# The head of a hybrid decoder step: rows of x scaled in place and turned by plain transposes, with another order of loads and of work

## The chip, the cores and the metric

The kernel runs on one core of a Trainium2 chip. Its engines run side by side, each through its own list in order: TensorE (PE, matrix products; PEld is its loading of stationary operands), VectorE (DVE), ScalarE (ACT), GpSimd (POOL) and SyncE (SP, which here only issues DMA transfers). The metric is the device time of one execution in microseconds (us). A profile shows one execution, with times counted from its span's start.

## The reference

One layer of a decoder on 1024 prompt rows and 8 x 8 sample rows, 1088 rows (T) of 1024 features in all. What matters here is its first part:

```python
mod = silu(c) @ w_ada + b_ada
shift, scale, gate = split(mod, 3)
h = rmsnorm(x, norm_g) * (1 + scale) + shift
proj = h @ w_in          # [u_pool | z_pool | z_ssm | xBC | dt | g]
...
x = x + gate * ((sigmoid(g_pool) * P + sigmoid(g_ssm) * S) @ w_o)
```

`c` has nine rows: one for the prompt and one for each of eight samples. P and S are the results of a pooling branch and a state-space branch, which take nearly all of the time and which the change leaves as they are.

## The kernel before

**Layout.** The work runs with features on partitions: h is held as eight tiles of 128 features by 1088 rows. The rows of x arrive as nine blocks (eight of 128 rows, and one of the 64 sample rows), so they are turned on the way. The blocks form three groups (XG), {0, 1}, {2, 3, 4} and {5 to 8}, with 256, 384 and 448 columns (BLK). "Feature k" below is a tile of 128 features, "group" one of these three sets of columns.

**The head**, `first()`, L838, does the following, and `in_line` (L340) pins the instructions of all five engines to the order in which the code writes them.
- x_load (L194) loads a block. x_square (L200) sums its squares, on DVE (L204) or ACT (L206). x_root (L208) takes the root of a group's mean squares on ACT, and x_unit (L212) the reciprocal rs on DVE; it then makes a diagonal matrix of each block's rs (L219, 128x128, DVE).
- x_turn (L223) multiplies a block of x, the stationary operand, by that diagonal, which scales and turns it in one fp32 product (L231), once per block and feature: 72 products. x_copy (L235) takes the result from PSUM to the tile `tf`, DVE for even features (L239) and ACT for odd ones (L241).
- ada_load, ada_mm, ada_out and ada_end (L252 to L300) make shift and scale, `md`, from w_ada in three parts: part 0 is for features 0 and 1, part 1 for 2 and 3, part 2 for 4 to 7. Each part is 64 products (L277), a copy on ACT (L284), transposes (L292) and sums on DVE (L296, L299).
- h_make (L309) forms h in a rounded high and a low half: hi on ACT (L323, for the sample columns L332), the scaled copy on DVE or ACT (L327, L325), low on DVE (L315).
- w_split (L850) splits a first weight tile into a high half (ACT, L163) and a low half (L166: on POOL, or on DVE where `V` is given). products (L856) multiplies it with h, three products per feature and tile (L866 to L868), into banks for the gates of columns t = 0 and 1.
- gate_bias and gate_load issue the loads for the last gate: a memset of bg on POOL (L827), four loads behind it on SP (L829), then weights (L817). gate_mm (L823) uses them.

**Behind the head.** `combine` (L466) makes the sums of h's quarters that the next products, a Strassen-like scheme (L595 to L597), use: three sums on DVE (L497 to L499), a rounding on ACT (L500), a low half on DVE (L493), for four features. `pair_w` (L527) does the like for weights: two loads (L529), differences on DVE (L540), splits on ACT and on DVE or POOL (L163, L166). `next(wst)` runs it one step on; its first step in the head holds two L540. `done` (L872) takes sigmoids of the gate columns on ACT (L875) and stores them, dt_block (L727, L730) the dt columns.

**What sets the order.** The written order within `first`; behind it a scheduler with priorities. SP issues loads in order as well, and a transfer waits for the one eight before it. PSUM tiles of kind "ps" come from five banks, those of kind "mm" from three.

Of the kernel before, what the change touches and what calls it, by code (L numbers as in the profile page):

```python
# [10 lines left out]
AF = mybir.ActivationFunctionType  # L11
ALU = mybir.AluOpType
# [8 lines left out]
P = 128  # L21
D = 1024
KT = D // P
# [30 lines left out]
def tile_pool_ssd_step(  # L54
# [6 lines left out]
    nc = tc.nc  # L61
# [37 lines left out]
    def R(shape=(P, T), dt=F32):  # L99
        return hs.tile(list(shape), dt, tag="R", name=nm("R"), bufs=3)  # L100
# [4 lines left out]
    def PB():  # L105
        return psB.tile([P, 512], F32, tag="ps", name=nm("ps"))
# [4 lines left out]
    def const(shape, name, dt=F32):  # L111
        return cp.tile(shape, dt, tag=name, name=name)
# [26 lines left out]
        nc.gpsimd.memset(rc[:, t:t + 1], 1.0 / (t + 1))  # L139


    c9 = const([P, KT, NB + 1], "c9")
    store_(c9, c_all)

# [8 lines left out]
    def c_turn():  # L153
        act(scT[:, :, 0:9], c9, AF.Silu)

    def v_turn():
        V.tensor_scalar(vT[:, 8:16], vT[:, 8:16], 1.0, None, ALU.add)
# [27 lines left out]
    xr = []  # L185
# [1 line left out]
    ss = const([P, 9], "ss")  # L187
    nc.gpsimd.memset(ss, 1.0)
    rs = const([P, 9], "rs")
    dg = []  # L190
    hh_ = [None] * KT
    hl_ = [None] * KT

# [6 lines left out]
    def x_square(i, eng):  # L200
        xt, n = xr[i]
        sqj = pa.tile([P, D], F32, tag="rawA", name=nm("sqj"), bufs=5)
        if eng is V:
            V.scalar_tensor_tensor(sqj[:n], xt[:n], 1.0, xt[:n], ALU.mult, ALU.mult, accum_out=ss[:n, i:i + 1])  # L204
        else:
            act(sqj[:n], xt[:n], AF.Square, accum_out=ss[:n, i:i + 1])  # L206

    def x_root(a, b):  # L208
        n = xr[a][1]
        act(rs[:n, a:b], ss[:n, a:b], AF.Sqrt, bias=eps[:n], scale=1.0 / D)  # L210

    def x_unit(a, b):  # L212
        n = xr[a][1]
        V.reciprocal(rs[:n, a:b], rs[:n, a:b])
        if not dg:
            dg.append(R())
        for i in range(a, b):
            n = xr[i][1]
            V.tensor_scalar(dg[0][:n, i * P:i * P + n], ident[:n, :n], rs[:n, i:i + 1], None, ALU.mult)  # L219

    tf = [None] * KT

    def x_turn(g3, k):  # L223

        if g3 == 0:
            tf[k] = tfp.tile([P, T], F32, tag="tf", name=nm("tf"), bufs=8)
        px = PB()
        c = 0
        for i in range((0, *XG)[g3], XG[g3]):
            xt, n = xr[i]  # L230
            mm(px[:, c:c + n], xt[:n, k * P:(k + 1) * P], dg[0][:n, i * P:i * P + n], start=True, stop=True)  # L231
            c += n
        return g3, k, px, c

# [8 lines left out]
    def x_turns(g3, ks):  # L243
        for k in ks:
            x_copy(x_turn(g3, k), nc.scalar if k % 2 else V)
# [6 lines left out]
    def ada_load(part, k):  # L252
        a, b = PARTS[part]
        w = (b - a) * P
        if part == 0:
            if k == 0:
                wtile[0] = Y4(hp, F32)
            t = wtile[0][:, k // 2, :D]
        else:
            if part == 2 or k % 2 == 0:  # L260
                wtile[part, k] = G((P, D))
            t = wtile[part, k if part == 2 else k - k % 2]
        if part == 2:
            load(t, w_ada[8 + k])
        else:
            if k % 2 == 0:
                load(t, w_ada[4 * part + k // 2])
            t = t[:, k % 2 * 512:k % 2 * 512 + 512]
        wraw[part, k] = t.rearrange("p (s c) -> p s c", s=2)
# [568 lines left out]
    def first():  # L838
        ET = mybir.EngineType
        every = (ET.PE, ET.Activation, ET.DVE, ET.Pool, ET.SP)  # L840
        in_line(every, True)
        raws = {}

        def w_load(t, j):
            raws[t, j] = raw_()
            load(raws[t, j], w_first[t, j].rearrange("p (k c) -> p k c", c=P))

        w = {}

        def w_split(t, j, eng=None):  # L850
            w[t, j] = split(raws[t, j], eng=eng)

        banks = {}

        def products(bi, ks):
            o, n = BLK[bi]  # L856
            for t in range(2):
                if (bi, t) not in banks:
                    banks[bi, t] = (PB if (bi, t) in ((1, 1), (2, 0), (2, 1)) else PA)()[:, :n]
            for k in ks:  # L860
                for t in range(2):
                    ps = banks[bi, t]
                    hi, lo = w[t, k // 4]
                    a, b = hi[:, k % 4, :], lo[:, k % 4, :]
                    rh, rl = hh_[k][:, o:o + n], hl_[k][:, o:o + n]
                    mm(ps, a, rh, start=(k == 0), stop=False)  # L866
                    mm(ps, b, rh, start=False, stop=False)
                    mm(ps, a, rl, start=False, stop=(k == KT - 1))  # L868

        tags = iter(("s1", "u2", "u3", "c2", "s1", "u2"))  # L870

        def done(bi, t):  # L872
            o, n = BLK[bi]
            buf = pa.tile([P, HF], F32, tag=next(tags), name=nm("g0"))
            act(buf[:, :n], banks[bi, t], AF.Sigmoid)  # L875
            store_(gs_d[t][:, o:o + n], buf[:, :n])

        for i in range(9):
            x_load(i)
        for k in range(KT):  # L880
            if k == KT - 2:
                w_load(0, 0)
                w_load(1, 0)
            ada_load(0, k)
        for k in range(KT):
            ada_load(1, k)
        for k in range(4):
            ada_load(2, k)
        late = late_loads()

        x_square(0, V)
        x_square(1, V)
        c_turn()
        x_root(0, 2)
        x_unit(0, 2)
        x_square(2, None)
        x_square(3, V)
        x_turns(0, range(2))
        x_square(4, None)
        x_turns(0, range(2, 4))  # L900
        x_root(2, 5)
        x_unit(2, 5)
        x_turns(0, range(4, 8))
        x_square(5, V)
        x_square(6, None)
        x_turns(1, range(4))
        x_square(7, V)
        x_square(8, None)
        x_turns(1, range(4, 6))
        x_root(5, 9)  # L910
        x_unit(5, 9)
        x_turns(1, range(6, 8))
        v_turn()
        x_turns(2, range(4))
        for k in range(6):
            ada_mm(0, k)
        x_turns(2, range(4, 5))
        w_split(0, 0)
        w_split(1, 0)
        ada_mm(0, 6)  # L920
        ada_mm(0, 7)
        mr = ada_out(0)
        x_turns(2, range(5, 6))
        ada_end(0, mr)
        turned = [x_turn(2, k) for k in (6, 7)]

        h_make(0, range(2))
        products(0, range(2))
        x_copy(turned[0], V)
        x_copy(turned[1], nc.scalar)  # L930
        h_make(1, range(2))
        for k in range(KT):
            ada_mm(1, k)
        products(1, range(2))
        h_make(2, range(2))
        w_load(0, 1)
        w_load(1, 1)
        for k in range(4, 8):
            ada_load(2, k)
        next(late)  # L940
        mr = ada_out(1)
        products(2, range(1))
        ada_end(1, mr)
        products(2, range(1, 2))

        for bi in range(2):
            h_make(bi, range(2, 4))
            products(bi, range(2, 4))
        h_make(2, range(2, 4))
        w_split(0, 1, V)  # L950
        w_split(1, 1, V)
        for k in range(KT):
            ada_mm(2, k)
        mr = ada_out(2)
        products(2, range(2, 3))
        ada_end(2, mr)
        products(2, range(3, 4))
        dtw = dt_w()
        run, (wz, wst) = light[0][1], light[0][0]()
        bg = gate_bias()  # L960
        for k in range(4):
            gate_load(k)
        next(wst)

        for bi in range(3):
            h_make(bi, range(4, 8))
        for bi in range(3):
            products(bi, range(4, 8))
            for k in range(2 * bi, min(2 * bi + 2, 4)):
                gate_mm(k)  # L970
                gate_load(k + 4)

        sums = combine()
        next(late)
        for bi in range(3):
            done(bi, 0)
            done(bi, 1)
            next(sums)
        dt_block(dtw, 0)
        dt_block(dtw, 1)  # L980
        next(sums)
        next(wst)
        dt_block(dtw, 2)
        next(sums)
        for k in range(4, 8):
            gate_mm(k)
        gate_end(bg)
        next(late, None)

        def hook(n):  # L990
            if n in (0, 2):
                next(wst)
            if n < 2:
                next(sums)
            if n in (3, 4):
                next(wst)
                next(sums)
        run(wz, hook)
        in_line(every)
# [1082 lines left out]
```

## Time and profile before

| | before |
|---|---|
| median of 3 runs | 1242.26 us (1239.66 to 1242.32) |
| span of the profiled execution | 1238.8 us |
| PE busy in 0 to 9 us | 0.00 us |
| PE busy in 20 to 40 us | 19.92 us |
| PE busy in 40 to 60 us | 18.44 us |
| PE busy in 77 to 100 us | 21.36 us |
| first turned block on PE (L231) | 9.29 us |
| shift and scale of part 0 on DVE (L296) | 30.37 us |
| first products of features 2 and 3 (L866) | 40.85 us |
| first large product (L595) | 77.73 us |

The profile gives the span of the one profiled execution; the time of a run lies some us above it. In a row of the timeline stand the start, the duration, the engine, the line, the operation and its tiles; a number x6 behind it says that several like instructions are joined, and the bracket gives the idle time of the engine ahead of the row and what ended it. A matmul's duration includes its way through the array, so that two in a row overlap; their pace is read from the starts. Rows of stretches give busy time and count, the granted clock of PE, the DMA share and GB/s. An fp32 product makes two records.

### The profile page before, as it was taken

Reading aid. Unit: us, or ns where it says so; the run is one execution under the profiler, and the core shown is the slowest. Engines: PE = TensorE matmul, PEld = TensorE weight load, DVE = VectorE, ACT = ScalarE, POOL = GpSimd, SP = SyncE. Lnnn points to the kernel's source line nnn. Section 1 sums busy time; section 2 is a strip of 40 time slices with the busy share of each in tenths; the row PEclk is TensorE's granted clock in tenths of the full one; section 3 lists DMA queues with packets and bytes.
Section 4 is the critical chain, followed back from the end, with each engine's and each line's share of the span. In section 5 each row is a group of like instructions: output and inputs, shape, how many; then the busy total and the mean of one; then the engine's idle time right before and its main releaser. Section 6 shows DMA issues by size and latency. Waiting matters only on the chain. (4 is left out here: it accounts for less than half of the span.)

```text
span 1238.8 us, 25381 instructions
## 1 busy us (share of the span) xinstructions
PE 1213.9 (98%) x9364; PEld 1145.0 (92%) x9364; DVE 909.2 (73%) x1579; ACT 692.8 (56%) x1611; POOL 678.0 (55%) x555
## 2 busy tenths in 40 slices
PE   6999999999999999999999999999999999999997
PEld 6779999999999999999898899999999999999786
DVE  4796688985989588975867775787767879666543
ACT  4665356565566556554554454877877768432111
POOL 1006669768898877774444465364565557456000
PEclk9999999999999999999999999999999999999999
DMA  9726445755556554453877775998665676485431
GB/s 363 290 99 226 145 161 148 188 190 170 164 173 208 158 168 146 169 179 114 251 248 211 231 223 183 329 306 298 192 203 176 195 228 198 143 296 167 153 111 51
DMA packets 183916, 243.25 MB, mean 196 GB/s; under 512 B 40808, under 2 KB 116912, under 8 KB 183792
## 3 DMA queue, kind: packets, MB, share of 16 engines
q1 hardware_dynamic: 132128, 167.90, 42.9%
q10 hardware_dynamic: 51664, 73.72, 17.6%
q8 instruction: 74, 1.21, 0.4%
q14 instruction: 50, 0.41, 0.1%
HBM read 166.96 MB, written 74.62 MB: 195 GB/s over the span
## 5 line engine op out<-in xcount | busy, mean ns | idle before, releaser
L166 POOL TENSOR_TENSOR wlo<-rawA,whi 128x512 fp32r<-128x512 f32 x120 | 187.5, 1569 | 143.1 <-DVE wlo L166 67.7
L166 POOL TENSOR_TENSOR wlo<-raw,whi 128x512 fp32r<-128x512 f32 x92 | 150.2, 1640 | 126.1 <-ACT whi L163 119.9
L360 PE MATMUL mm<-Y,whi 128*128 128x352 f32 (+1 forms) x480 | 160.1, 334 | 0.6
L361 PE MATMUL mm<-Y,whi 128*128 128x352 f32 (+1 forms) x480 | 157.1, 327 | 0.4 <-DVE Y L1485 0.4
L362 PE MATMUL mm<-Y,wlo 128*128 128x352 f32 (+1 forms) x480 | 157.1, 327 | 0.0
L595 PE MATMUL mm<-Y,whi 128*128 128x272 f32 x496 | 144.5, 292 | 1.0 <-ACT whi L163 0.8
L597 PE MATMUL mm<-Y,wlo 128*128 128x272 f32 x496 | 143.5, 290 | 1.3 <-DVE wlo L166 0.8
L596 PE MATMUL ps<-Y,whi 128*128 128x272 f32 x496 | 143.2, 289 | 0.0
L595 PE MATMUL ps<-Y,whi 128*128 128x272 f32 x496 | 142.8, 288 | 0.0
L597 PE MATMUL ps<-Y,wlo 128*128 128x272 f32 x496 | 142.8, 288 | 0.0
L596 PE MATMUL mm<-Y,whi 128*128 128x272 f32 x496 | 142.5, 287 | 0.0
L1031 DVE SCALAR_TENSOR_TENSOR GA<-GA,cvT,GA 128x1112 f32<-128x1112 f32 x72 | 128.4, 1786 | 0.7 <-ACT GA L1028 0.5
L163 ACT ACTIVATE whi<-rawA 128x512 fp32r<-128x512 f32 x125 | 77.8, 626 | 90.4 <-PE ps L596 51.1
L163 ACT ACTIVATE whi<-raw 128x512 fp32r<-128x512 f32 x96 | 58.7, 626 | 83.0 <-DVE raw L540 38.2
L595 PEld LDWEIGHTS mm<-Y,whi 128*128 128x128 f32 x496 | 93.6, 189 | 4.6 <-issue 2.4
L597 PEld LDWEIGHTS mm<-Y,wlo 128*128 128x128 f32 x496 | 93.1, 188 | 3.0 <-DVE wlo L166 1.2
L595 PEld LDWEIGHTS ps<-Y,whi 128*128 128x128 f32 x496 | 93.4, 188 | 1.7 <-issue 0.8
L596 PEld LDWEIGHTS mm<-Y,whi 128*128 128x128 f32 x496 | 93.5, 188 | 0.8 <-issue 0.6
L360 PEld LDWEIGHTS mm<-Y,whi 128*128 128x128 f32 x480 | 90.2, 188 | 4.1 <-DVE G L1861 2.3
L596 PEld LDWEIGHTS ps<-Y,whi 128*128 128x128 f32 x496 | 93.3, 188 | 0.2
L597 PEld LDWEIGHTS ps<-Y,wlo 128*128 128x128 f32 x496 | 93.2, 188 | 0.0
L361 PEld LDWEIGHTS mm<-Y,whi 128*128 128x128 f32 x480 | 90.2, 188 | 2.6 <-DVE Y L1485 0.9
(422 smaller groups left out, 3727.0 us busy)
## 6 DMA issues: line engine op xcount, KB each, us to landing
rawA<-in_w_in SPq DMA_DIRECT2D x62, 512.0 KB
dec<-acs_d SPq DMA_DIRECT2D x32, 512.0 KB
xbc<-GA ACTq DMA_DIRECT2D x24, 512.0 KB
xb<-xbc SPq DMA_DIRECT2D x32, 384.0 KB
pw<-in_w_ssm_out ACTq DMA_DIRECT2D x32, 256.0 KB
ws<-ph ACTq DMA_DIRECT2D x32, 256.0 KB
ws<-pw SPq DMA_DIRECT2D x32, 256.0 KB
hs<-in_state_turned SPq DMA_DIRECT2D x32, 256.0 KB
```

The costliest lines, as they stand in the source:

```text
L163: ins = act(hi[:, :, :ncols], raw[:, :, :ncols], AF.Copy)
L166: (eng or nc.gpsimd).tensor_tensor(lo[:, :, :ncols], raw[:, :, :ncols], hi[:, :, :ncols].bitcast(F32), ALU.subtract)
L360: mm(ps[:, :n], a, rh[k][:, o:o + n], start=(k == 0), stop=False)
L361: mm(ps[:, :n], a, rl[k][:, o:o + n], start=False, stop=False)
L362: mm(ps[:, :n], b, rh[k][:, o:o + n], start=False, stop=(k == nk - 1))
L595: mm(p, hi, ah, start=(k == 0), stop=False)
L596: mm(p, hi, al, start=False, stop=False)
L597: mm(p, lo, ah, start=False, stop=(k == 3))
L1031: V.scalar_tensor_tensor(d[:, :n], rp[:, k:k + n], cvT[:, 24 * k + mc:24 * k + mc + 1], d[:, :n], ALU.mult, ALU.add)
```

## The change

1. x_unit makes no diagonals. A new helper, x_scale, multiplies a block of x by rs where it stands (128x1024): blocks 0, 2, 5 and 7 on DVE, 1, 4 and 8 on ACT, 3 and 6 on POOL. x_turn then uses transposes with the identity.
2. PE begins with 20 products of the identity with itself. A square root of eps on ACT stands ahead of the first x_root.
3. Loads: x 0 and 1, part 0 of w_ada, x 2 to 4, the first weights, x 5 to 8, part 1, the second weights, part 2.
4. The order of the head: group 0 is turned, part 0 of shift and scale made, and group 0's h and products for features 0 and 1; then group 1 in the same way, then part 1 and group 2.
5. w_split of the second weight tiles has no `V` any more, so its low halves go to POOL, and they stand ahead of the memset of bg.
6. `next(wst)` stands behind h_make of features 4 to 7 instead of ahead of it.

```diff
     def x_unit(a, b):
         n = xr[a][1]
         V.reciprocal(rs[:n, a:b], rs[:n, a:b])
-        if not dg:
-            dg.append(R())
-        for i in range(a, b):
-            n = xr[i][1]
-            V.tensor_scalar(dg[0][:n, i * P:i * P + n], ident[:n, :n], rs[:n, i:i + 1], None, ALU.mult)
+
+    def x_scale(i, eng):
+        xt, n = xr[i]
+        if eng is None:
+            act(xt[:n], xt[:n], AF.Copy, scale=rs[:n, i:i + 1])
+        else:
+            eng.tensor_scalar(xt[:n], xt[:n], rs[:n, i:i + 1], None, ALU.mult)
...
-            mm(px[:, c:c + n], xt[:n, k * P:(k + 1) * P], dg[0][:n, i * P:i * P + n], start=True, stop=True)
+            nc.tensor.transpose(px[:, c:c + n], xt[:n, k * P:(k + 1) * P], ident[:n, :n])
...
-        for i in range(9):
+        warm = PB()
+        for _ in range(20):
+            mm(warm[:, :P], ident, ident, start=True, stop=True)
+        x_load(0)
+        x_load(1)
+        for k in range(KT):
+            ada_load(0, k)
+        for i in range(2, 5):
+            x_load(i)
+        w_load(0, 0)
+        w_load(1, 0)
+        for i in range(5, 9):
             x_load(i)
         for k in range(KT):
-            if k == KT - 2:
-                w_load(0, 0)
-                w_load(1, 0)
-            ada_load(0, k)
-        for k in range(KT):
             ada_load(1, k)
+        w_load(0, 1)
+        w_load(1, 1)
...
         c_turn()
+        act(eps_root, eps, AF.Sqrt)
         x_root(0, 2)
         x_unit(0, 2)
+        x_scale(0, V)
+        x_scale(1, None)
+        x_turns(0, range(8))
+        for k in range(KT):
+            ada_mm(0, k)
+        v_turn()
+        mr = ada_out(0)
         x_square(2, None)
+        ada_end(0, mr)
+        h_make(0, range(2))
         x_square(3, V)
-        x_turns(0, range(2))
         x_square(4, None)
-        x_turns(0, range(2, 4))
+        w_split(0, 0)
+        w_split(1, 0)
         x_root(2, 5)
         x_unit(2, 5)
-        x_turns(0, range(4, 8))
+        x_scale(2, V)
+        x_scale(3, nc.gpsimd)
+        x_scale(4, None)
+        products(0, range(2))
         x_square(5, V)
+        x_turns(1, range(2))
+        x_turns(1, range(2, 4))
+        h_make(1, range(2))
         x_square(6, None)
-        x_turns(1, range(4))
+        x_turns(1, range(4, 6))
+        products(1, range(2))
         x_square(7, V)
         x_square(8, None)
-        x_turns(1, range(4, 6))
         x_root(5, 9)
         x_unit(5, 9)
         x_turns(1, range(6, 8))
...
+        x_scale(5, V)
+        x_scale(6, nc.gpsimd)
+        x_scale(7, V)
+        x_scale(8, None)
         for k in range(KT):
             ada_mm(1, k)
...
+        mr = ada_out(1)
+        x_turns(2, range(2))
+        ada_end(1, mr)
+        h_make(2, range(2))
+        x_turns(2, range(2, 4))
+        products(2, range(2))
         next(late)
...
+        x_turns(2, range(4, 8))
...
-        w_split(0, 1, V)
-        w_split(1, 1, V)
+        w_split(0, 1)
+        w_split(1, 1)
...
-        next(wst)
 
         for bi in range(3):
             h_make(bi, range(4, 8))
+        next(wst)
```

Lines of the changed kernel stand two higher than before behind L189: L233 is the turn, L325 the hi, L542 the differences, L597 the large product. Its scales are L219 (ACT) and L221 (DVE, POOL).

**ACT, from the copy of part 0's products to the second group's scale.** In the changed kernel these rows follow one another; Y_129 and Y_130 hold the blocks of x, sqj takes squares, whi_384 and whi_388 are the first weights' high halves, Y_372 is h's high half.

```order
L286 ACTIVATE mr_363<-ps_329 128x128
L206 ACTIVATE sqj_365,ss<-Y_129 128x1024
L325 ACTIVATE Y_372<-tf_289,md 128x256
L325 ACTIVATE Y_372<-tf_294,md 128x256
L327 ACTIVATE tf_294<-tf_294,md 128x256
L206 ACTIVATE sqj_382,ss<-Y_130 128x1024
L164 ACTIVATE whi_384<-raw_250 128x512
L164 ACTIVATE whi_388<-raw_252 128x512
L210 ACTIVATE rs<-ss,eps 128x3
L219 ACTIVATE Y_130<-Y_130,rs 128x1024
```

Before, the squares and the root of group 1 stood among the copies of group 0, ahead of the weight splits and of the copy mr; now they stand behind it, around group 0's h, and the weight splits stand ahead of the root.

**POOL, all of its work in the head** of the changed kernel; the wlo are low halves of the first and the second weights, the Y are blocks 3 and 6 of x.

```order
L167 TENSOR_TENSOR wlo_385<-raw_250,whi_384 128x512
L167 TENSOR_TENSOR wlo_389<-raw_252,whi_388 128x512
L221 TENSOR_SCALAR Y_129<-Y_129,rs 128x1024
L221 TENSOR_SCALAR Y_130<-Y_130,rs 128x1024
L167 TENSOR_TENSOR wlo_656<-raw_267,whi_655 128x512
L167 TENSOR_TENSOR wlo_660<-raw_269,whi_659 128x512
L829 MEMSET bg 128x256
```

Before, the first two and the memset were the whole of it; two scales and two low halves, which DVE made, now stand between them.

**DVE, from the last low halves of h into combine.** In the changed kernel (G are h's halves of features 4 to 7, L499 to L501 the first three sums of combine, whose last one ACT waits for):

```order
L317 TENSOR_TENSOR G_746<-tf_319,G_745 128x448
L317 TENSOR_TENSOR G_751<-tf_324,G_750 128x448
L542 TENSOR_TENSOR raw_788<-rawA_720,rawA_718 128x512
L542 TENSOR_TENSOR raw_789<-raw_788,rawA_718 128x512
L499 TENSOR_TENSOR tf_309<-tf_289,tf_309 128x544
L542 TENSOR_TENSOR raw_1314<-rawA_1298,rawA_1296 128x512
L500 TENSOR_TENSOR tf_289<-tf_289 128x544
L542 TENSOR_TENSOR rawA_1296<-rawA_1296 128x4x128
L501 TENSOR_TENSOR tf_289<-tf_309,tf_289 128x544
```

Before, two of the differences (L540 there) stood right behind part 2's shift and scale, ahead of the first row of h, and two among h's sample columns (L330, L331); no difference stood between the last low half and the first L499. All four now stand there.

More of the change, by code (lines that the diff above doesn't have):

```diff
@@ L139, in tile_pool_ssd_step @@
         nc.gpsimd.memset(rc[:, t:t + 1], 1.0 / (t + 1))
+    eps_root = const([P, 1], "eps_root")
     c9 = const([P, KT, NB + 1], "c9")
@@ L189, in tile_pool_ssd_step @@
     rs = const([P, 9], "rs")
-    dg = []
     hh_ = [None] * KT
@@ L912, in first @@
         x_turns(1, range(6, 8))
[L913 to L931, printed above, removed]
+        x_scale(5, V)
+        x_scale(6, nc.gpsimd)
+        x_scale(7, V)
+        x_scale(8, None)
         for k in range(KT):
             ada_mm(1, k)
[L934 to L937, printed above, removed]
         for k in range(4, 8):
             ada_load(2, k)
+        mr = ada_out(1)
[4 more added lines that the diff above has]
+        products(2, range(2))
         next(late)
[L941 to L944, printed above, removed]
+        x_turns(2, range(4, 8))
         for bi in range(2):
```

## The prediction

> **What bounds the kernel now.** I read the busy times first, then what TensorE (PE) waits for, then the first 80 us engine by engine.
>
> ```profile
> span 1238.8 us, 25381 instructions
> PE 1213.9 (98%) x9364; PEld 1145.0 (92%) x9364; DVE 909.2 (73%) x1579; ACT 692.8 (56%) x1611; POOL 678.0 (55%) x555
> ...
> PE ps L231 <- DVE R L219: 9.3, 1, 9.3
> PE ps L1188 <- DVE dec L1232: 2.3, 1, 2.3
> ...
> PE mm L595 <- ACT whi L163: 0.8, 2, 0.4
> ```
>
> PE is busy for 98% of the span. Its one long wait is the 9.3 us before the first turned block. After that the longest is 2.3 us, far behind the head, for DVE work on a result of PE. So a delay of PE in the head comes back at the end almost whole, and a gain too, provided that the engines that feed PE arrive as much earlier. The second thing to see is how close they run behind it:
>
> ```profile
> 9.29 12.27 PE L231 MATMUL ps<-R,Y 128*128 128x128 f32 x86 [9.29 <-DVE R L219]
> ...
> 25.53 1.52 PE L277 MATMUL ps<-Y,scT 128*32 128x128 f32 x48
> ...
> 40.85 0.38 PE L866 MATMUL mm<-Y,whi 128*128 128x256 f32 x1
> 45.63 3.66 PE L277 MATMUL ps<-G,scT 128*32 128x256 f32 x64
> 56.63 0.64 PE L823 MATMUL ps<-R,scT 128*32 128x256 f32 x8
> 76.70 0.61 PE L823 MATMUL ps<-gk,scT 128*32 128x256 f32 x8
> 77.73 0.39 PE L595 MATMUL mm<-Y,whi 128*128 128x272 f32 x1 [0.41 <-ACT whi L163]
> 78.57 0.39 PE L597 MATMUL mm<-Y,wlo 128*128 128x272 f32 x1 [0.33 <-DVE wlo L166]
> ```
>
> These PE rows are the places I follow. The head proper ends at 40.85, where the products of features 2 and 3 begin; the first large product begins at 77.73 (L595), and **there PE already waits for ACT and DVE**, by 0.41 and 0.33 us. So up to 77.73 two chains arrive together: PE's own work, and the chain DVE, ACT, weights. The change has to be judged on both, and the later of them counts.
>
> **The head, step 1: PE's savings.** A block is turned by a true transpose instead of an fp32 product:
>
> ```profile
> 22.71 0.43 PE L231 MATMUL ps<-R,R 64*128 64x64 f32 x2
> ...
> 23.94 0.43 PE L231 MATMUL ps<-R,R 64*128 64x64 f32 x2
> ...
> 672.85 0.60 PE L1226 MATMUL ps<-ident,hst 128*64 128x128 f32 x4
> ```
>
> One feature of the last group (three full blocks and a short one) takes 23.94 - 22.71 = 1.23 us. Four fp32 transposes take 0.60, of which 0.27 is the tail of one by the groups (272 ns), so 0.11 each and 0.44 for such a feature. Eight features save 6.3 us there. Then the clock:
>
> ```profile
> 9.00:11.50 2.50, 2.21 (x10) 1.00 1.03 418
> ...
> 13.60:14.60 1.00, 1.00 (x10) 1.00 1.01 229
> 1233.00:1235.50 2.50, 0.00 (x0) 1.00 0.00 0
> 1235.70:1238.80 3.10, 0.00 (x0) 0.50 0.44 169
> ```
>
> Ten records take 2.2 us at 9 to 11.5 and 1.0 us at 13.6. A full block makes two records, so at full rate it takes 0.2 as a product and 0.11 as a transpose: the 40 blocks of the first two groups save 4 us. And PE begins at half rate for some 4.4 us, which the 20 warm-up products move into the wait (about ten at 0.43 and ten at 0.22, 6.5 us; once ident is made, at about 2.1, they run until 8.7, as the first scaled rows arrive). That saves 2.2 us. The last rows: the granted clock holds to 1235.5 with no matmul, and is 0.50 from 1235.7, some 3.4 us after the last of them. In all some 12 us of PE time go. They help only if the chain that feeds PE is as much shorter.
>
> **Step 2: the chain that feeds it.** I set the changed order's rows end to end, each from the later of its engine and its operands, at these durations:
>
> ```profile
> 8.62 1.04 ACT L206 ACTIVATE sqj<-Y 128x1024 f32<-128x1024 f32 x1
> ...
> 26.07 1.14 ACT L163 ACTIVATE whi<-raw 128x512 fp32r<-128x512 f32 x2
> ...
> 30.88 1.09 ACT L323 ACTIVATE Y<-tf,md 128x256 fp32r<-128x256 f32 x2 [0.23 <-DVE md L296]
> ...
> 33.07 1.29 ACT L323 ACTIVATE Y<-tf,md 128x384 fp32r<-128x384 f32 x2
> ...
> 40.20 1.10 ACT L323 ACTIVATE Y<-tf,md 128x256 fp32r<-128x256 f32 x2 [1.74 <-DVE md L296]
> ```
> ```profile
> 26.78 2.50 POOL L166 TENSOR_TENSOR wlo<-raw,whi 128x512 fp32r<-128x512 f32 x2 [23.58 <-ACT whi L163]
> ...
> L1167 POOL TENSOR_SCALAR_AFFINE_SELECT dec<-dec 128x1024 f32<-128x1024 f32 x32 | 34.9, 1092 | 41.5 <-ACT cE L1376 29.8 <-DMA gs<-u 11.4 <-DMA dec<-acs_d 0.3
> L1699 POOL TENSOR_TENSOR m<-m,m 128x1024 fp32r<-128x1024 f32 x2 | 4.9, 2437 | 4.1 <-issue 2.3 <-DMA half<-in_x_sample 1.8
> ...
> L1986 DVE TENSOR_SCALAR q<-q,sso 128x640 f32<-128x640 f32 x1 | 0.6, 553 | 0.1
> 30.37 0.18 DVE L296 TENSOR_TENSOR md<-ps,vT 128x18 f32<-128x18 f32 x1 [1.43 <-PE ps L292]
> ```
>
> - Group 0 and part 0 are early: 16 transposes (1.8 us) from 8.8, the 64 part products (1.52 for 48, so 2.0), and shift and scale (md) at about 13.5 instead of 30.37.
> - Then **ACT's written order** rules. Behind md stand, one after another: h hi (1.1) and scaled copy (0.6) of group 0 with the square sums of blocks 2 (before) and 4 (behind, each about 1.15 with its read-out), the two weight splits (1.14), and the root (0.3): from 13.0 to about 18. POOL's two weight remainders (2.5) begin at 17.4, with the first whi, and end at 19.9. So PE sits still from 13.2 to 17.4, 4.2 us, longer than the 3.4 after which the clock fell above; the products of group 0 then run at half rate, to 21.8.
> - x_scale of block 3 stands on POOL behind them. The trace has no such operation; its nearest rows are POOL's one-input 128x1024 at 1.09 and its two-input at 2.44. I take 1.3, near the first. On DVE the scaling lies between 0.55 (128x640) and the square sum's 1.2; I take 0.8. Group 1 turns at 21.8, its products run at about 24.6 to 27.3.
> - ACT again: two copies, hi (1.29) and scaled copy, a square sum, a copy, a square sum, the root, ends at 28.8; then reciprocal, one copy and two scales on DVE, to 30.9. Group 2's first two features turn, md of part 1 comes at 32.5, h and products of group 2 fill until 37, and four features of group 2 follow at the pace of the copies. The last copy ends at 40.6.
>
> The next h of features 2 and 3 begins on ACT then, against 40.20. Set end to end in the same way, the order of before comes out 0.6 us early at its PE row 40.85, so like against like the head is **1.0 us later**, not earlier: the 12 us of PE time have become waits.
>
> **Step 3: POOL beside DVE.** Weight remainders and two scales now run on POOL while DVE scales and squares:
>
> ```profile
> 670.76 4.89 DVE L540 TENSOR_TENSOR raw<-rawA,rawA 128x512 f32<-128x512 f32 x1
> 671.62 1.28 POOL L166 TENSOR_TENSOR wlo<-raw,whi 128x512 fp32r<-128x512 f32 x1
> ...
> 674.08 1.09 POOL L1171 TENSOR_SCALAR_AFFINE_SELECT dec<-dec 64x512 f32<-64x512 f32 x1
> ```
>
> A DVE difference that takes 0.69 alone stood for 4.89 us while POOL ran four operations in a row. In the new head DVE's scale of block 2 and a square sum meet POOL's string (at 18 to 21), and the scales of blocks 5 and 7 meet POOL's of block 6 (1.3). If each side only waits at a place where something else is later, this costs 0; if DVE is held both times, 0.8 + 1.0. I take the middle, **0.9**. The Trainium skill, "SBUF — State Buffer", section "Who interferes with whom", speaks of the same thing: VectorE and GpSimd share one port pair as an exclusive lock, and `tensor_scalar` in its two-port mode takes it. By that rule all of the 1.8 would be paid, and the sum would be 4.5; the row above agrees with a lock for a two-input operation, and no row quoted shows it for a scaling.
>
> **Step 4: the differences (L540) lose their cover.**
>
> ```profile
> 51.41 0.68 DVE L540 TENSOR_TENSOR raw<-rawA,rawA 128x512 f32<-128x512 f32 x1
> ...
> 60.67 0.68 DVE L540 TENSOR_TENSOR rawA<-rawA 128x512 f32<-128x512 f32 x1
> ...
> 65.21 0.72 DVE L497 TENSOR_TENSOR tf<-tf,tf 128x544 f32<-128x544 f32 x1
> ...
> 75.10 0.72 DVE L493 TENSOR_TENSOR Y<-tf,Y 128x544 fp32r<-128x544 f32 x1
> 67.55 0.66 ACT L500 ACTIVATE Y<-tf 128x544 fp32r<-128x544 f32 x1 [0.41 <-DVE tf L499]
> ...
> 77.06 1.14 ACT L163 ACTIVATE whi<-rawA 128x512 fp32r<-128x512 f32 x2
> ```
>
> Before, four of them lie between 51.41 and 61.3. The first two run while DVE would wait for ACT's hi anyway; the others hold up the sample columns by their 0.68 each, at most. Now all four stand between the last h (ahead of 65.21) and the first L499, and ACT's L500 waits for that row (0.41 <-DVE). ACT's list is written in order: the gates, their stores, dt and the weight split at 77.06 queue behind L500, and PE at 77.73 waits for that split. DVE runs without a wait from 65.21 to the sum at 75.10, so it cannot hide them there. Four at a pitch of about 0.6 cost 2.4 us; about 0.7 comes back because h is no longer interrupted. Net **+1.7**.
>
> **Sum.** Head 1.0, POOL beside DVE 0.9, differences 2.4 - 0.7: the product at 77.73 comes 3.6 us later. PE's own delay of 1.9 lies inside it. Behind that PE is busy throughout, and what it waits for is made from its own results, so the rest shifts whole. The profiled execution has its span of 1238.8 alone; the median of the runs, 1242.26, is 3.5 above it, and I add the difference there: 1242.26 + 3.6 = **1245.9 us**. The bounds of the terms: head 0 (all scales cheap, the clock kept) to 2.2 (POOL at 2.44), contention 0 to 1.8, differences 1.4 to 2.1 (pitch 0.6 to 0.7, less 0.7 to 1.0); together +1.4 to +6.1. None of them can fall below nothing: an operation is not made faster by a neighbour, and a difference costs DVE its time wherever it stands.
>
> **Rivals.**
> 1. *The head does run ahead* (faster, 0.10). The 12 us of PE time are real. If the ACT and POOL chain of step 2 is shorter than I think and half of them is kept, part 2's products, at 45.63 now, start at 39.6: 6 us sooner, less 1.7 for the differences, 1238 us. Its price turns on the last copy of group 2: my 40.6 has to become 37.0 for no change, 34.5 for a gain of 0.2% (2.5 us, about what a measurement of this kernel can tell from no change). For it: the loads of part 0 now stand ahead of those of seven x blocks. Against: three stretches in a row in which ACT has no slack.
> 2. *The clock stays at half through the head* (slower, 0.12). The long wait at 13.2 and waits of 2 to 3 us behind it might keep PE at half rate until 40. PE's work from 17 to 41 is then about 14 us at full rate (56 transposes at 0.11, 36 products at 0.12 to 0.2, 64 part products) and 28 at half, in a stretch of 24: 4 us more, 1250. The Trainium skill, "TensorE: Matmul & The Clock Gate", Part 4 (PE-mode transpose), speaks for it: transposes don't count as PE-busy in the same way, so 72 of them would not keep the gate open where fp32 products did; no run here shows that yet.
> 3. *Nothing net* (0.20): the differences fall into waits that I don't see, or the head gains 2 us: 1242 to 1244.
> 4. *Late gate weights* (slower, 0.06):
>
> ```profile
> 41.94 2.31 SPq L829 DMA_DIRECT2D bg<-in_b_ada  x4
> ```
>
> The splits of the second weights now stand on POOL ahead of the memset of bg, at about 48 to 51, so this load and the gate weights behind it on SP go 9 us later, and the products at 56.63 could wait 1 to 3 us. Up to 1.7 of that hides behind the DVE chain; 1246 to 1248.
>
> **Numbers.** Forecast 0.52, the rivals 0.10, 0.12, 0.20, 0.06. Of the forecast 0.05 falls within 0.2%: slower 0.65, same 0.25, faster 0.10. The forecast's own range is 1243.7 to 1248.4; the range 1241.3 to 1250.5 takes in rivals 3 and 4 and most of 2, and leaves out rival 1 and the far end of 2.
>
> **What would show it.** Step 1: L233 at 0.11 a block, begun before 9.3. Step 2: md of part 0 near 13.5, PE idle for 3 to 5 us behind it with ACT or POOL as releaser, half rate in the products after it, and the products of features 2 and 3 at 41 to 43. Step 3: DVE scales over 1 us beside POOL. Step 4: the four L542 rows (L540 now) between L317 and L501, the first L502 on ACT 3 to 4 us later than 67.55, and a PE wait of 1.5 to 2.5 us ahead of L597. I am wrong if part 2's products start before 45, or if the wait ahead of L597 doesn't grow.

## The result and the profile after

The changed kernel takes **1249.64 us** (median of 4 runs, 1249.08 to 1251.02) against 1241.15 before (4 runs, 1239.66 to 1242.32). The ratio is 1.0072, with a 95% interval of 1.0058 to 1.0087: **slower by 8.9 us** (7.2 to 10.8) by the ratio; the medians are 8.5 apart. It was forecast slower, at 1245.9, within 1241.3 to 1250.5. The direction held, and the time lies inside that range, near its upper end, but above the forecast's own range (1243.7 to 1248.4); the forecast loss of 3.6 us was less than half of the real one.

| | before | after | forecast |
|---|---|---|---|
| span of the profiled execution | 1238.8 | 1249.3 | |
| shift and scale of part 0 on DVE | 30.37 | 13.47 | 13.5 |
| turns of group 1, past block 3 | | 24.60 | 21.8 |
| turns of group 2, past block 6 | | 36.03 | 30.9 |
| products of features 2 and 3 | 40.85 | 48.24 | 42.8 |
| first dt product on PE | 68.07 | 75.43 | |
| first large product | 77.73 | 85.54 | 81.3 |

What PE waited for in the changed kernel (total, times, longest):

```profile
PE mm L868 <- ACT whi L164: 4.3, 1, 4.3
PE ps L233 <- POOL Y L221: 2.7, 2, 1.5
...
PE mm L869 <- POOL wlo L167: 1.4, 2, 0.8
PE mm L597 <- ACT whi L164: 1.3, 2, 0.9
PE mm L868 <- ACT Y L325: 1.1, 1, 1.1
```

The 9.3 us of waiting ahead of the first turned block are filled with the warm-up products (the first turn starts at 8.60, for 9.29 before). New are the expected wait of 4.3 us for the first weight split, and 2.7 us for POOL's scales, which the forecast did not have as a wait. The head on POOL and DVE, by the timeline, shows why:

```profile
17.81 2.94 POOL L167 TENSOR_TENSOR wlo<-raw,whi 128x512 fp32r<-128x512 f32 x2 [14.60 <-DMA raw<-in_w_first]
20.73 3.82 POOL L221 TENSOR_SCALAR Y<-Y,rs 128x1024 f32<-128x1024 f32 x1
32.76 3.21 POOL L221 TENSOR_SCALAR Y<-Y,rs 128x1024 f32<-128x1024 f32 x1 [8.21 <-DVE rs L214]
55.05 2.53 POOL L167 TENSOR_TENSOR wlo<-raw,whi 128x512 fp32r<-128x512 f32 x2 [19.08 <-ACT whi L164]
```
```profile
18.83 0.79 DVE L221 TENSOR_SCALAR Y<-Y,rs 128x1024 f32<-128x1024 f32 x1
19.55 2.29 DVE L204 SCALAR_TENSOR_TENSOR sqj<-Y 128x1024 f32<-128x1024 f32 x1
...
33.03 2.06 DVE L221 TENSOR_SCALAR Y<-Y,rs 128x1024 f32<-128x1024 f32 x2
```

POOL's scale of block 3 takes **3.82 us** and that of block 6 **3.21**, where 1.3 was reckoned, 2.44 at most. The first ends at 24.55, when PE's turns go on (24.60 below). Then PE's own rows:

```profile
17.78 0.58 PE L868 MATMUL mm<-Y,whi 128*128 128x256 f32 x1 [4.34 <-ACT whi L164]
...
24.60 3.89 PE L233 MATMUL ps<-ident,Y 128*128 128x128 f32 x17 [1.51 <-POOL Y L221]
...
36.03 0.44 PE L233 MATMUL ps<-ident,Y 128*128 128x128 f32 x2 [1.16 <-POOL Y L221]
...
48.24 0.39 PE L868 MATMUL mm<-Y,whi 128*128 128x256 f32 x1 [1.12 <-ACT Y L325]
```

Seventeen transposes take 3.89 us, about 0.22 each, twice the 0.11 at full rate. The granted clock of the stretches (the number behind the five engines' columns and ahead of DMA share and GB/s) says the same:

```profile
14.00:20.00 6.00, 1.45 (x4) 1.00 (x4) 3.75 (x8) 5.31 (x10) 2.19 (x2) 0.75 1.04 388
20.00:30.00 10.00, 7.72 (x31) 6.41 (x31) 4.29 (x7) 3.21 (x6) 4.55 (x2) 0.50 1.03 365
30.00:40.00 10.00, 8.83 (x98) 6.83 (x97) 7.05 (x18) 5.79 (x12) 3.21 (x1) 0.84 0.87 319
```

Half rate was expected in the products of group 0 only. Behind the head, the four differences stand where the order put them, and ACT's list follows:

```profile
71.97 0.68 DVE L542 TENSOR_TENSOR raw<-rawA,rawA 128x512 f32<-128x512 f32 x1
...
75.23 0.69 DVE L542 TENSOR_TENSOR rawA<-rawA 128x512 f32<-128x512 f32 x1
75.83 0.72 DVE L501 TENSOR_TENSOR tf<-tf,tf 128x544 f32<-128x544 f32 x1
83.10 0.58 ACT L732 ACTIVATE dts<-mm,dtb 128x384 f32<-128x384 f32 x1 [0.50 <-DMA gs<-g]
84.31 0.66 ACT L502 ACTIVATE Y<-tf 128x544 fp32r<-128x544 f32 x1 [0.63 <-DVE tf L501]
85.54 0.39 PE L597 MATMUL mm<-Y,whi 128*128 128x272 f32 x1 [0.87 <-ACT whi L164]
```

And the two rows of before to compare with:

```profile
66.72 0.72 DVE L499 TENSOR_TENSOR tf<-tf,tf 128x544 f32<-128x544 f32 x1
75.52 0.58 ACT L730 ACTIVATE dts<-mm,dtb 128x384 f32<-128x384 f32 x1 [1.98 <-DMA gs<-g]
```

L501 comes 9.1 us later than L499 did before, but the large product only 7.8 (77.73 there). DVE's last low half of h was 6.8 us late (71.43 for 64.67), so the differences added 2.4. ACT's wait for the gates' stores, 1.98 us ahead of the same dts before, is down to 0.50: it took up most of the 2.4.

### The profile page after: what moved, and what is told of

Read it like the earlier page. It is cut to its first block, busy times and chain, and to the rows that moved or that the text cites. A ratio compares the mean times of both kernels' runs of the same rounds, so it can differ in the third digit from the quotient of the medians.

```text
span 1249.3 us, 25321 instructions
## 1 busy us (share of the span) xinstructions
PE 1221.0 (98%) x9332; PEld 1147.4 (92%) x9332; DVE 913.0 (73%) x1572; ACT 696.4 (56%) x1615; POOL 688.4 (55%) x559
## 5 line engine op out<-in xcount | busy, mean ns | idle before, releaser
L167 POOL TENSOR_TENSOR wlo<-rawA,whi 128x512 fp32r<-128x512 f32 x120 | 190.2, 1591 | 125.9 <-ACT whi L164 71.1
L597 PE MATMUL mm<-Y,whi 128*128 128x272 f32 x496 | 144.4, 291 | 2.2 <-ACT whi L164 1.3
L597 PE MATMUL ps<-Y,whi 128*128 128x272 f32 x496 | 142.9, 288 | 0.7 <-ACT s L642 0.7
L597 PEld LDWEIGHTS mm<-Y,whi 128*128 128x128 f32 x496 | 93.6, 189 | 5.8 <-issue 3.1
L597 PEld LDWEIGHTS ps<-Y,whi 128*128 128x128 f32 x496 | 93.4, 188 | 2.6 <-ACT s L642 1.0
```

Of the source, the lines that this page charges most:

```text
L167: (eng or nc.gpsimd).tensor_tensor(lo[:, :, :ncols], raw[:, :, :ncols], hi[:, :, :ncols].bitcast(F32), ALU.subtract)
L597: mm(p, hi, ah, start=(k == 0), stop=False)
```

## The experiments

Twelve runs were made: of ten edited kernels, one of them twice, and of the changed kernel once more. The ratios are to the kernel before on the same chip in the same set; each set has its own median for it (1239.19, 1240.55 and 1240.84 us).

### POOL's scales on DVE

```diff
-        x_scale(3, nc.gpsimd)
+        x_scale(3, V)
...
-        x_scale(6, nc.gpsimd)
+        x_scale(6, V)
```

> The changed kernel with the scales of blocks 3 and 6 on DVE instead of POOL, nothing else. Theory A (POOL's scale, 3.8 and 3.2 us where 1.3 was reckoned, stands on the chain of both groups): the turns of group 1 begin about 2.4 us sooner (22.2 for 24.6), those of group 2 another 1 to 1.5 sooner, the products of features 2 and 3 at about 44.5 for 48.2, the time about 1246. Theory B (the half clock in the head is what costs, whatever feeds it): the chain is shorter, but PE at half rate takes the place of the wait; the products of features 2 and 3 not before 47, the time 1248.5 to 1249.5.

1246.89 us, ratio 1.0057 (1.0043 to 1.0071). In its profile group 1 turns at 22.55, group 2 is past its last wait for a scale at 33.19, and the products of features 2 and 3 come at 43.38, 4.9 us sooner than in the changed kernel. So the chain is A's. The median fell by less than A forecast, so the kernel was run again, beside the changed kernel itself:

> The changed kernel once more, on the same chip as the next three, so that they can be compared with it: 1249 to 1251 if the first measurement holds, with the products of features 2 and 3 at 46 to 49 us.

> The changed kernel with POOL's two scales on DVE, once more beside the changed kernel itself. Its profile had the products of features 2 and 3 4.9 us sooner but its median was only some 2 us lower. If the 4.9 us are real and part of them is given back at random by the clock: 2.5 to 4.5 us less than the changed kernel in the same set. If the head's gain is not carried to the end: under 1.5 us.

The changed kernel: 1250.65 us, ratio 1.0081 (1.0068 to 1.0094). With the scales on DVE: 1246.79, ratio 1.0046 (1.0033 to 1.0060). The scales on POOL cost **3.9 us** by the medians of this set, 4.3 by the ratios; by the first pair, from two sets, 1.9 by the ratios. So the size is some 2 to 4 us and no closer. The second profile of the changed kernel had the products of features 2 and 3 at 46.20, two us ahead of the first. The clock of group 2's products differs (0.50 from 39.6 to 43.9 us in the first profile, 1.00 from 40 to 46 in the second, where the products behind 46.20 run at half rate instead). At the first large product 0.8 us of the two are left (84.75 for 85.54). Where the clock falls differs between executions of one kernel, and a single profile of this head is good to some 2 us.

### What a scale on POOL costs by itself

```diff
         x_scale(4, None)
+        probe = [pa.tile([P, D], F32, tag="rawA", name=nm("probe"), bufs=5) for _ in range(2)]
+        nc.gpsimd.tensor_scalar(probe[0], xr[2][0], rs[:, 2:3], None, ALU.mult)
+        nc.gpsimd.tensor_scalar(probe[1], xr[2][0], 0.5, None, ALU.mult)
```

> The changed kernel with two more scales of a 128x1024 block on POOL right behind that of block 3, into tiles that nobody reads: the first by the column rs as there, the second by the constant 0.5. If the operation itself has the price (3.2 to 3.8 us with a column): 3.2 or more for the first, with DVE idle or copying from PSUM beside it, and about 1.1 for the second if the column makes it dear, 3.2 if not. If DVE beside it made it dear (contention): 1.1 to 1.5 for both.

POOL's timeline of this kernel, and DVE beside the two probes:

```profile
20.60 3.81 POOL L221 TENSOR_SCALAR Y<-Y,rs 128x1024 f32<-128x1024 f32 x1
24.40 2.84 POOL L927 TENSOR_SCALAR probe<-Y,rs 128x1024 f32<-128x1024 f32 x1
27.22 2.77 POOL L928 TENSOR_SCALAR probe<-Y 128x1024 f32<-128x1024 f32 x1
```
```profile
25.19 0.56 DVE L241 COPY tf<-ps 128x384 f32<-128x384 f32 x1 [3.49 <-PE ps L233]
26.47 0.56 DVE L241 COPY tf<-ps 128x384 f32<-128x384 f32 x1 [0.72 <-PE ps L233]
```

The first probe has only copies from PSUM beside it on DVE and takes 2.84 us; the constant saves nothing (2.77). So neither named alternative fits: about **2.8 us is the operation's own**, with a column or without. In place it takes 0.4 (block 6) to 1.0 (block 3) more, where DVE scales or squares beside it; that this company is the reason is likely but not shown apart (the probes also write to tiles of their own). Most of the price is not contention.

### The differences back in their place

```diff
         for k in range(4):
             gate_load(k)
+        next(wst)
 
         for bi in range(3):
             h_make(bi, range(4, 8))
-        next(wst)
```

> The changed kernel with the first step of the pair's differences (four rows on DVE) back ahead of the h of features 4 to 7. Step 4 of the prediction (they cost 1.7 net): about 1248.0. Rival (most of it falls into a wait of ACT for the stores of the gates that was there before, 2.0 us at 75.5): the first large product only 0.4 to 0.5 us sooner, about 1249.2.

1249.65 us, ratio 1.0085 (1.0071 to 1.0099): **no gain at all**, against the 1.7 us of step 4; the rival's 0.4 to 0.5 us are too small for these runs to tell. Its DVE rows show a reason that neither had:

```profile
56.66 0.68 DVE L542 TENSOR_TENSOR raw<-rawA,rawA 128x512 f32<-128x512 f32 x1
...
64.90 0.22 DVE L332 TENSOR_TENSOR tf<-tf,md 128x64 f32<-128x64 f32 x1
67.63 0.69 DVE L542 TENSOR_TENSOR raw<-rawA,rawA 128x512 f32<-128x512 f32 x1 [2.51 <-DMA rawA<-in_w_in]
```
```profile
55.70 1.39 SPq L831 DMA_DIRECT2D bg<-in_b_ada  x4
...
58.95 1.67 SPq L531 DMA_DIRECT2D rawA<-in_w_in  x3
```

In its old place the third difference now waits 2.51 us for a transfer, in the middle of h. That transfer is issued on SP at 58.95, behind the bg loads at 55.70, which wait for the memset that POOL makes behind the second low halves; before, the like transfers were issued at 47.82. So the move of the differences and the queue behind POOL hang together: with late loads the old place is no better than the new one.

### The move of the differences alone, on the kernel before

The same four lines, the other way round, in the kernel before.

> The kernel before with that one step moved behind the h of features 4 to 7, nothing else. Step 4 of the prediction: 1.7 us slower than before, about 1243. Rival (hidden in ACT's wait for the gates' stores): 0 to 0.5 us slower, with that wait shortened and the first large product at 77.7 to 78.2.

1241.01 us, ratio 1.0010 (1.0001 to 1.0019): 1.2 us slower, 0.1 to 2.4. In its profile the head runs 0.58 us later from the first turns on, by no doing of the edit, and the large product is 1.18 later, so about 0.6 is the edit's. ACT's waits for the stores shrink from 2.0 to 0.9 us, as the rival had it. By the profile the rival's 0.5 is nearer than the 1.7 of step 4; by the runs both lie inside the interval.

### Warm-up products alone

```diff
+        warm = PB()
+        for _ in range(20):
+            mm(warm[:, :P], ident, ident, start=True, stop=True)
         for i in range(9):
             x_load(i)
```

> The kernel before with only the 20 warm-up products added. If PE's own pace sets the end of the old head, the 2.2 us of half rate are saved: the products of features 2 and 3 at 38.7 for 40.85, and the time about 1239. If the chain of ACT, DVE and the loads sets it: no more than 0.5 us gained.

1237.86 us, ratio 0.9986 (0.9978 to 0.9995): 1.7 us **faster** than before. Its profile has the products of features 2 and 3 at 38.98. PE's pace does set the old head, and the warm-up is worth about what step 1 gave it (2.2 us of PE time; 0.6 to 2.7 measured).

### Filling PE's waits

```diff
         ada_end(0, mr)
+        fill(18)
...
         products(0, range(2))
+        fill(8)
...
         mr = ada_out(1)
+        fill(4)
```

`fill(n)` makes n products of the identity with itself into a PSUM tile of their own.

> The changed kernel with products of the identity with itself put into three waits of PE in the head (18 behind the transpose of part 0, 8 behind the products of group 0, 4 behind the 64 products of part 1), so that PE is kept busy; their results are not used. Theory B (the half clock costs about 3 of the 7.4 us by which the head is late): the products of groups 0, 1 and 2 run at 0.11, 0.17 and 0.20 us a step instead of 0.21 to 0.37, the products of features 2 and 3 come at about 45 for 48.2, the time is 1246 to 1247. Theory A (POOL's scales alone set the head): PE waits longer instead, features 2 and 3 at 47.5 or later, no more than 0.7 us gained.

1250.20 us, ratio 1.0070 (1.0054 to 1.0085), where the changed kernel had 1.0072 and 1.0081. The profile does what B says, at first: 17 transposes take 2.08 us at 24.52, not 3.89, and the products of features 2 and 3 start at 45.04. But half rate comes back right behind, from 46.2 to 49.5, among products that PE makes without a pause (busy time and count, clock, DMA share, GB/s):

```profile
46.20:49.50 3.30, 3.30 (x15) 0.50 0.02 6
```

And the time does not fall. The half clock goes with the late head; keeping it out of the three waits did not repair the time.

### The change's core in the old order

```diff
         x_unit(2, 5)
+        x_scale(2, V)
+        x_scale(3, V)
+        x_scale(4, None)
...
-            mm(px[:, c:c + n], xt[:n, k * P:(k + 1) * P], dg[0][:n, i * P:i * P + n], start=True, stop=True)
+            nc.tensor.transpose(px[:, c:c + n], xt[:n, k * P:(k + 1) * P], ident[:n, :n])
```

> The kernel before, its order and its loads, with the 20 warm-up products, and with the scaling in place and the plain transposes, all scales on DVE (0, 2, 3, 5, 7) and ACT (1, 4, 6, 8), none on POOL. If the loads of part 0, which land last at 22 to 23 us, set the old head once PE is quicker: the same as with the warm-up products alone, shift and scale of part 0 at 27.5 to 28.5, about 1237.5 to 1238.5. If PE's own work still sets it: 10 us of it are gone, and features 2 and 3 start 3 to 6 us sooner, 1233 to 1235. If transposes let the clock fall: half rate in the products of the head, 1239 to 1241.

1238.50 us, ratio 0.9985 (0.9975 to 0.9994), the same as with the warm-up alone. The transpose of part 0 stands on PE at 28.39 and the products of features 2 and 3 start at 38.97, as there (28.12 and 38.98). Scaling in place and plain transposes thus cost nothing, and in the old order gain nothing more. Part 0's first products start at 24.21, no sooner than with the warm-up alone (23.64). The loads of part 0, the bound of the first theory, are not the reason: PE has no wait ahead of these products, and in the last experiment below they start at 22.77. One reason is the scaling, for which PE now waits (total, times, longest; 0.5 us in all for the diagonals with the warm-up alone):

```profile
PE ps L232 <- DVE Y L220: 4.9, 4, 1.9
```

The clock is the other, in stretches of this kernel's head:

```profile
12.00:14.00 2.00, 0.11 (x1) 1.00 1.07 330
14.00:16.00 2.00, 1.69 (x12) 0.92 1.00 320
16.00:18.00 2.00, 2.00 (x12) 0.50 1.01 406
...
20.00:22.00 2.00, 1.50 (x8) 1.00 1.04 414
22.00:24.00 2.00, 2.00 (x10) 0.62 1.02 406
24.00:26.00 2.00, 2.00 (x37) 0.52 1.05 414
26.00:28.00 2.00, 2.00 (x43) 1.00 1.01 401
```

From 9.75 to 24.2 PE makes nothing but transposes. The clock falls at 16 while they run, behind a wait of 1.9 us, is up again at 20, and falls once more at 22 to 26. The Trainium skill, "TensorE: Matmul & The Clock Gate", Part 4 (PE-mode transpose), says that transposes don't count as PE-busy in the same way. That the clock falls among them agrees; that it came back at 20, behind transposes alone, does not agree with their counting for nothing.

### All repairs together, with and without the filling

```diff
-        x_scale(3, nc.gpsimd)
+        x_scale(3, V)
...
-        x_scale(6, nc.gpsimd)
+        x_scale(6, V)
...
-        w_split(0, 1)
-        w_split(1, 1)
+        w_split(0, 1, V)
+        w_split(1, 1, V)
...
+        next(wst)
 
         for bi in range(3):
             h_make(bi, range(4, 8))
-        next(wst)
```

> The changed kernel with four repairs together: the scales of blocks 3 and 6 on DVE, the filling products of the run before this one in three waits of PE, the differences ahead of the h of features 4 to 7 again, and the second weights' low halves on DVE again (so that the memset of bg and the loads behind it go earlier). If the terms found so far add up (about 3 for POOL's scales, 3 for the clock, 0.5 to 1 for the differences): 1240 to 1242, the same as before or up to 2 us slower. If they overlap (each hides the other): 1244 or more.

> The repaired kernel without the filling products: POOL's scales on DVE, the differences ahead of the h of features 4 to 7, the second weights' low halves on DVE. If the differences and the queue behind POOL cost 0.5 to 1.5 together once the loads for them are no longer late: 1 to 1.5 us less than the run before this one, and within 1 us of the repaired kernel with filling. If the filling was what brought the repaired kernel down: 1246 to 1247, as the run before.

With filling 1245.91 us, ratio 1.0042 (1.0026 to 1.0059); without it, in the other set, 1244.42, ratio 1.0035 (1.0021 to 1.0048). The filling brings nothing, for the second time. Beside the kernel with the scales alone (1246.79 in the same set) the differences and the queue together take 2.4 us off the median, 1.4 by the ratios; the intervals overlap, so the size is loose. What remains is **4.3 us (2.6 to 6.0) slower than before**. Besides the order of the head and its loads this kernel keeps the warm-up, the scaling in place and the transposes, which together gained 1.9 us in the old order (0.9985 above). Against that kernel the ratios are 6.2 us apart. Not all of it is the head's: in this kernel's profile PE is 2.4 us later than in the profile of before from 240 to 585 us, 1.4 at 750 and 3.4 at the end; some 2.1 us arise between the last two (see the part on the prediction).

### Transposes for the last group only

```diff
-        for i in range(a, b):
+        for i in range(a, min(b, 5)):
             n = xr[i][1]
             V.tensor_scalar(dg[0][:n, i * P:i * P + n], ident[:n, :n], rs[:n, i:i + 1], None, ALU.mult)
...
+            if g3 == 2:
+                nc.tensor.transpose(px[:, c:c + n], xt[:n, k * P:(k + 1) * P], ident[:n, :n])
+                c += n
+                continue
...
         x_unit(5, 9)
+        x_scale(5, V)
+        x_scale(6, None)
+        x_scale(7, V)
+        x_scale(8, None)
```

This is the kernel before, with the warm-up products, in its old order.

> The kernel before with the warm-up products, and with the scaling in place and plain transposes for the last group alone (blocks 5 and 7 on DVE, 6 and 8 on ACT); groups 0 and 1 keep the diagonals. If PE's work sets the old head: 5.8 us of it go, of which the loads of part 0 (landing at 22 to 23) leave 1 to 2: shift and scale of part 0 at 26.5 to 27, 1 to 2 us less than the warm-up alone (0.25 to 0.3% below before). If the transposes let the clock fall or the loads set all: the same as with the warm-up alone, 0.15% below.

**1237.16 us, ratio 0.9971** (0.9960 to 0.9983): 3.6 us faster than before, and the lowest ratio of all, though its interval touches that of the warm-up alone (0.9978 to 0.9995). The short blocks, dear as products (a feature of the last group takes 1.23 us), are cheap as transposes (0.68, from 20.53 to 21.21). With fp32 products in the first two groups the clock stays up (1.00 from 0 to 40 us; mean of the span 0.999, against 0.990 in the changed kernel). But behind the warm-up PE also has no wait above 0.74 us in this head, so what keeps the clock up, products or the lack of waits, is not separated; shift and scale of part 0 start on PE at 26.16 instead of 30.00, and the products of features 2 and 3 at 36.74.

## Why the prediction was right, and where its sizes were off

- **The number.** 1249.64 lies above the forecast's own range and inside the wide one, which takes in most of rival 2 (1250). That it does is partly luck. In the loss stand one term that was mis-sized, POOL's scale, and slower products far behind the head, which the sum put at nothing; to these comes half rate beyond the products of group 0, which the sum left to rival 2 and whose share the runs don't show. The expected signs show the same: the products of features 2 and 3 at 48.24 for 41 to 43, the first L502 on ACT 9.1 us later (76.64 for 67.55) and not 3 to 4, PE's wait ahead of L597 0.87 and not 1.5 to 2.5.
- **The bound** (two chains that arrive together at the large product, PE's own work and the chain through DVE and ACT): right. PE is 7.4 us late at the first dt product (75.43 for 68.07), and the wait for the other chain adds 0.5 to that (0.87 for 0.41).
- **"The rest shifts whole"** behind that: not quite. PE is 7.8 us late at the large product, 8.5 from 235 to 585 us and 10.5 at the end of this profile. Some 2.1 us of that arise in two stretches in which the products themselves are slower. The same 257 products of the last projection, from 1175 to 1230 us in the profile of before, take 54.78 us from the first start to the last in all five profiles of the old order, and 55.74 in all nine of the new one; from 760 to 1050 us the difference is 1.1 (289.8 for 290.9, and 290.0 in one of the five). PE makes the same products in the same order, and the clock is 1.00 in both. One group of the last projection before, and the same after, from 1150 us on (count, busy us, mean ns):

```profile
L1973 PE MATMUL ps<-m,G 128*128 128x512 f32 x26 | 10.1, 389 | 0.0
L1983 PE MATMUL ps<-m,G 128*128 128x512 f32 x30 | 11.8, 395 | 0.0
```

How late the head is plays no part: the repaired kernels have the same 55.74. The cause is open. What the nine kernels share and the five lack is the order of the head and of its loads, and one more constant tile (eps_root); no run separates them. In some profiles of either order there is also a step of 1.5 us near 1084 us, where the clock falls (0.83 from 1080 to 1090 us with the warm-up alone); it is in neither of the two profiles compared here.
- **Step 1** (12 us of PE time): right in kind. The 16 turns of group 0 take 2.23 us from 8.60 (1.8 from 8.8 reckoned), and the warm-up is worth 1.7 us alone. The 4 us for 40 blocks are 3.6 by the prediction's own 0.2 and 0.11. That the rest becomes waits was right too.
- **Step 2**: the order of events was right: md at 13.47, 4.3 us of PE waiting, then POOL, then ACT. The term that was mis-sized is POOL's scale, taken at 1.3 between 1.09 and 2.44. It measures 2.8 by itself and 3.2 to 3.8 in place, and costs some 2 to 4 us of the total. Rows of other operations of the same shape had bounded it, and the operation lay outside both. The order itself, reckoned at 1.0, is 4.3 (2.6 to 6.0) by the repaired kernel, of which some 2.1 are, by the profiles, the slower products above. Why the rest is still more than 1.0 was not taken apart further: in that kernel's profile the products of features 2 and 3 stand at 44.91, with the clock at 0.60 from 38 to 41, but with the waits filled they stood at 43.23 and the time was no better.
- **Step 3** (0.9 for POOL beside DVE): a real effect, but its price was put in the wrong place. DVE's square takes 2.29 us for 1.22, two of its scales 2.06, as much as three without POOL beside them (2.07 in the kernel with the scales on DVE and ACT alone), some 1.7 us together. That delays nothing: behind the square DVE waits 3.49 us for PE, and both scales are done ahead of POOL's. What counts is that POOL takes 0.4 to 1.0 more. By the rule of the Trainium skill, "SBUF — State Buffer", section "Who interferes with whom", a scale in the two-port mode would wait for the whole of POOL's operation. The rows of block 6 don't show that: both DVE scales are done at 35.09, POOL's scale, which began 0.27 us ahead of them, at 35.97. Beside a two-input operation of POOL, in the kernel with the scales of blocks 3 and 6 on DVE, one scale seems held to its end:

```profile
18.90 1.72 POOL L167 TENSOR_TENSOR wlo<-raw,whi 128x512 fp32r<-128x512 f32 x1
19.41 1.75 DVE L221 TENSOR_SCALAR Y<-Y,rs 128x1024 f32<-128x1024 f32 x1
```

It takes 1.75 us for 0.75, and ends 0.5 us behind POOL's operation.
- **Step 4** (differences, 1.7 net): the mechanism is there and by the profile the size was too big. Alone it costs about 0.6 by the profile, 1.2 us (0.1 to 2.4) by the runs, which leave the 1.7 open. The step that failed is that DVE's delay passes through ACT undiminished: ACT had a wait of 2.0 us for the gates' stores, and the delay filled it first.
- **The rivals.** The second, half rate through much of the head, came true beside the forecast and not in place of it (clock 0.75, 0.50 and 0.84 in the stretches above); its price in the time could not be shown, since filling did not lower it. The fourth was wrong about who waits: the gate products at 63.99 had no wait in the changed kernel. The late queue on SP held up the weights of the differences where these were put back, and took away the gain. Rivals 1 and 3 did not happen.

## What to carry to other kernels

A row of the same shape on the same engine is no bound for another operation there: 1.09 and 2.44 us were taken as the bounds of a scale that takes 2.8. Where such an operation lands on the chain between two engines, measure it alone before moving it. And a saving on the busiest engine pays only as far as its feeders keep up: transposes for one group and the warm-up gained 3.6 us in the old order (1.7 by the warm-up alone), and transposes were part of a loss of 8.9 in an order that made PE wait for ACT and POOL. Compare profiles to the end of the program too: 2.1 us of the loss lie 650 us and more behind the part that was edited, where nothing was meant to change. Before moving work into an idle engine's list, look at what is queued behind it on every queue it feeds.

## What the hardware showed beyond that

- POOL's multiplication of 128x1024 fp32 by a column or a constant takes 2.77 to 2.84 us, more than its product of two tensors of that shape in the profile of before (2.44), and 3.7 times DVE's 0.75 for the same scale.
- PE's granted clock falls at points where PE is busy with transposes (0.50 from 16 to 18 us in the old order with transposes everywhere, with 2.00 us of 2.00 busy). It falls among products without a pause as well (0.50 from 46.2 to 49.5 us in the filled kernel, 3.30 us of 3.30 busy).
- The same products can be slower in another kernel at a clock of 1.00: 217.8 ns from start to start on average in the last projection of the new order, 214.0 in the old.
- Where the clock falls differs between executions of one kernel: the products of features 2 and 3 came at 48.24 us in one profile of the changed kernel and at 46.20 in another.
